# A gated two-mixer block on one core: new places in the queues for modulations, split weights and gate loads, and the long convolution's differences taken from a PSUM copy

## The chip, the cores and the metric

One core of a Trainium2 chip. The metric is the device time of one execution in microseconds; of the kernel before there are three, 1468.36, 1468.63 and 1471.03 us, median 1468.63. The engines are PE (TensorE, matrix products), DVE (VectorE), ACT (ScalarE), POOL (GpSimd) and SP (SyncE, which here only starts DMAs). Each engine takes its instructions in order from its own queue.

## The reference

The block takes x (1024 positions by 1024 channels) and a condition c. Cut to what matters:

```python
mod = silu(c) @ w_ada + b_ada                       # sh1, sc1, g1, sh2, sc2, g2
h = rms_norm(x, norm_mix_g) * (1 + sc1) + sh1
b_s, c_s, v_s, v_c, gl_c, gate_br = split(h @ w_in) # 7 x 1024 columns
y_a = (b_s * causal_dwconv(c_s * v_s, conv_short_w)) @ w_short_out   # 3 taps
u = causal_dwconv(v_c * sigmoid(gl_c), conv_conf_w) + conv_conf_b    # 31 taps
y_b = silu(layer_norm(u, conf_ln_g, conf_ln_b)) @ w_conf_out
g_a, g_b = split(sigmoid(gate_br))
x = x + g1 * ((g_a * y_a + g_b * y_b) @ w_o)
h2 = rms_norm(x, norm_ffn_g) * (1 + sc2) + sh2
a, bgate = split(h2 @ w_ffn_in)
x = x + g2 * ((silu(a) * bgate) @ w_ffn_out)
return rms_norm(x, final_norm_g)
```

## The kernel before

Channels lie on the 128 partitions, positions along the free axis, in halves of 512 columns (`H`). Every matrix product is done in fp32r with a high and a low part of each operand, in three matmuls: high by high, low by high, high by low (L504, L505, L507). A weight is loaded by SP into one of five `raw` buffers (pools `rawp` and `rawbp`), `split_w` casts it to `wh` on ACT (L243) and subtracts to get `wl` on DVE or POOL (L244); there are three buffers of each, so a weight can be split about two products ahead of its use. Loads of raw wait for the split that last used the buffer.

Products come in groups of seven, named "1265734" in that order (a scheme that replaces eight block products by seven, with sums of blocks). Each product is 24 matmuls into two PSUM banks, which ACT and DVE then evacuate ("evac"): ACT copies those of "1", "6" and "5", DVE adds or multiplies those of "2", "7", "3" and "4".

The stages in time:

- The input projection, to about 570 us, in 18 "duals" `d`, each of seven products that yield two streams of 128 channels (`PAIRS`: u, p, q and g streams). Beside it run, on DVE: the long convolution, eight blocks `j` of 45 taps each (`conv`, from dual 1 to dual 12); the short convolution (`short_conv`, L854 on ACT and L857 on DVE), whose steps for the p streams of one dual are issued late, in the next dual, and work in a PSUM bank `x` that is the next dual's `z`, needed first by its product "5"; and modulations (`modulation_of`, L485), each a reduction over a 128x1024 block of w_ada that SP loads, two in each of the duals 3 to 9, at the products named in `MOD_AT`.
- `w_short` products (to about 648 us), then the `w_conf` products, in the order `CONF_ORDER`, which interleaves two groups `d`; their operands `z1` to `z7` are made tile by tile from `cv` by `z_first`, `z_5`, `z_6` and so on: DVE forms `t2z`, ACT casts it to `z6h`, DVE subtracts to `z6l`. The weights of "5", "7" and "3" are sums of two blocks, made by a DMA that accumulates onto `raw` from POOL's queue (`add` in `conf_units`, L397); that of "6" is summed on DVE (L407). On the same POOL queue `gates_b` loads gate tiles `gb` (L1421), and finished tiles go out from it by the accumulating `ma<-gb` (L1394).
- `w_o` and the feed-forward part, which the change does not touch.

The long convolution of block j: `ev` and `od` are the even and odd positions of `u[j]`, `d = ev - od` and `e` the same shifted by one (tile `diff`, one buffer, L1149 and L1150). It gathers odd taps into PSUM accumulators `a0` and `a1` (tiles `c0`, `c1`, two buffers in all), then 15 taps on `e` into c1, and 16 on `d` into c0. Each tap is pinned behind the evac of a product by `read_at(conv_at(...))`. When a block is done, `add_conv` adds it into `tot` on POOL (L1189).

The order on an engine is set by a list scheduler; `tc.issue_after(ins)` pins what is issued within it behind the named instruction in that order.

Of the kernel before, what the change touches and what calls it, by code (L numbers as in the profile page):

```python
# [38 lines left out]
ALU = mybir.AluOpType  # L39
# [4 lines left out]
H = 512  # L44
# [23 lines left out]
BEGUN = 2  # L68
# [33 lines left out]
GATED = 10  # L102


CONV_FROM, CONV_DUALS = 1.0, 11.06

# [8 lines left out]
PRODUCTS = "1265734"  # L117
# [2 lines left out]
CONF_ORDER = [(d, m) for m in "1256" for d in range(2)] + [(0, "3")] + [(d, m) for m in "74" for d in range(2)] + [(1, "3")]  # L120


MOD_FROM, MOD_AT = 16, "53"

# [12 lines left out]
def block_kernel(ctx: ExitStack, tc: tile.TileContext, x0, xT, c, vecs, ada, w_first, w_plain, w_duals,  # L139
                 w_short, w_conf, w_o, w_fi, w_fo0, w_fo1, outT):  # L140
    nc = tc.nc
# [16 lines left out]
    rawp = pool("raw", 3)  # L158
# [8 lines left out]
    rawbp = pool("raw_b", 2, side="right")  # L167
# [4 lines left out]
    def ps2_tile(name):  # L172
        return ps2p.tile([P, H], F32, tag="ps2", name=name)
# [205 lines left out]

        return {m: (lambda m=m: unit(m)) for m in PRODUCTS}  # L380

    conf_homes = [rawp, rawbp, rawp]

    def conf_units(mats, d):


        a = {}
        mat = dict(zip(("11", "12", "21", "22"), mats))

        def get(b, home=None):  # L390
            if home is None:
                conf_homes.append(conf_homes.pop(0))
                home = conf_homes[-1]
            return load(mat[b], home=home)

        def add(raw, b):
            nc.gpsimd.dma_start(raw, mat[b], accum_op=ALU.add)  # L397
            return raw

        def unit(m):  # L400
            if m == "5":
                raw = a["s1"] = add(get("22"), "21")
            elif m == "6":
                lo = split_w.lo
                raw = a["s2"] = get("11", (rawp, rawbp)[d])
                with tc.issue_after(lo):
                    nc.vector.tensor_tensor(raw, raw, a["s1"], ALU.add)  # L407
            elif m == "7":
                raw = add(get("21"), "11")
            elif m == "3":  # L410
                raw = add(a["s2"], "12")
            else:
                raw = get({"1": "11", "2": "12", "4": "22"}[m])
            return split_w(raw, 1024)

        return {m: (lambda m=m: unit(m)) for m in PRODUCTS}

# [432 lines left out]
    def short_conv(j, p, banks):  # L850

        sc[j] = uc_tile(f"sc{j}", T)
        for h, ps in enumerate(banks):
            nc.scalar.activation(ps, p[:, h * H : (h + 1) * H], AF.Copy, scale=col(V_SW, j))  # L854
        for h, ps in enumerate(banks):
            for s in range(1, SK):
                nc.vector.scalar_tensor_tensor(  # L857
                    out=ps if s < SK - 1 else sc[j][:, halves[h]], in0=p[:, h * H + s : (h + 1) * H + s],
                    scalar=col(V_SW + s * KC, j), in1=ps, op0=ALU.mult, op1=ALU.add,
                )  # L860


    reads = []

    def plus(out, ps, b):
        plus.ins = nc.vector.tensor_tensor(out, ps, b, ALU.add).ins
# [16 lines left out]
    def win_evac(d, pairs, banks):  # L883

        st = [{} for _ in pairs]

        def start(e, kind, j):
            if kind == "u":
                u.append(u_tile(j))
                e["b"] = [u[j][:, CK - 1 + h * H : CK - 1 + (h + 1) * H] for h in range(2)]  # L890
            elif kind == "p":
                e["p"] = uc_tile(f"p{j}", T + SK - 1)
                nc.vector.memset(e["p"][:, : SK - 1], 0.0)
                e["b"] = [e["p"][:, SK - 1 + h * H : SK - 1 + (h + 1) * H] for h in range(2)]
            else:
                e["b"] = [None, g_tile("v")]

        def begin():

            rows = uc_tile("sig", T)  # L900
            for i, e in enumerate(st):
                e["t"] = uc_tile("sig", T)
                e["b"], e["c"] = [None, rows[:, halves[i]]], [e["t"][:, s] for s in halves]
                nc.sync.dma_start(e["c"][0], part_dram[d, i])

        def bring(i):
            nc.scalar.copy(banks["x", i], st[i]["c"][0])

        def evac(i, m, ps):
            plus.ins = None  # L910
            read(i, m, ps)
            if plus.ins:
                late_by = 2 * max(0, d - GATED + 1)
                reads.append((d + (2 * (PRODUCTS.index(m) - late_by) + i + 1) / (2 * len(PRODUCTS)), plus.ins))

        def read(i, m, ps):
            kind, j, *rest = pairs[i]
            e = st[i]
            if m in "165":
                if m == "5":  # L920
                    e["z"] = e["c"][1] if kind == "g" else g_tile("z")
                copy = nc.scalar.copy({"1": banks.get(("y", i)), "6": e.get("b", [0, 0])[1], "5": e.get("z")}[m], ps)
                if i:
                    run_late(copy.ins)
            elif m == "2":
                start(e, kind, j)
                if kind == "q":
                    times(sc[j][:, halves[0]], ps, sc[j][:, halves[0]])
                else:
                    nc.scalar.copy(e["b"][0], ps)  # L930
            elif m == "7":
                z = banks["y", i] if kind == "q" else e["z"]
                plus(z, ps, e["z"])
                if kind == "g":
                    late.append(lambda: nc.scalar.activation(z, z, AF.Sigmoid, scale=-1.0))
                elif kind == "q":
                    minus_times(sc[j + 1][:, halves[1]], z, sc[j + 1][:, halves[1]])
            elif m == "3":
                b, z = e["b"][1], e["z"]
                if kind == "u":  # L940
                    nc.scalar.activation(z, z, AF.Sigmoid, scale=-1.0)
                plus(b if kind == "g" else ps, ps, b)
                if kind == "u":
                    times(b, ps, z)
                elif kind == "p":
                    minus_times(b, ps, z)
                elif kind == "q":
                    times(sc[j][:, halves[1]], ps, sc[j][:, halves[1]])
                else:
                    late.append(lambda: nc.scalar.activation(b, b, AF.Sigmoid))  # L950
            elif kind == "u":
                nc.scalar.activation(ps, ps, AF.Sigmoid, scale=-1.0)
                times(e["b"][0], ps, e["b"][0])
            elif kind == "p":
                minus_times(e["b"][0], ps, e["b"][0])
                late.append(lambda: short_conv(j, e["p"], [banks["x", p] for p in range(2)]))
            elif kind == "q":
                minus_times(sc[j + 1][:, halves[0]], ps, sc[j + 1][:, halves[0]])
                for n in range(2):
                    q_store(j + n)  # L960
            else:
                nc.scalar.activation(e["c"][0], ps, AF.Sigmoid, scale=-1.0)
                def store():
                    nc.scalar.dma_start(gate_dram[j][:, halves[1]], e["b"][1])
                    nc.scalar.dma_start(gate_dram[rest[0]], e["t"])
                late.append(store)
        evac.begin, evac.bring = begin, bring
        return evac
# [163 lines left out]
    def conv_at(j):  # L1132
        return CONV_FROM + j * CONV_DUALS / KC
# [5 lines left out]
    def read_at(t):  # L1139

        return max((r for r in reads if r[0] <= t), key=lambda r: r[0])[1]

    def conv(j):
        eo = u[j].rearrange("p (n two) -> p n two", two=2)
        ev, od = eo[:, :, 0], eo[:, :, 1]
        diff = diffp.tile([P, T + CK - 1], F32, tag="diff", name="diff")
        d, e = diff[:, :NE], diff[:, NE : 2 * NE - 1]
        with tc.issue_after(read_at(conv_at(j))):
            nc.vector.tensor_tensor(d, ev, od, ALU.subtract)  # L1149
            nc.vector.tensor_tensor(e, ev[:, 1:], od[:, : NE - 1], ALU.subtract)  # L1150
        a0, a1 = ps2_tile("c0"), ps2_tile("c1")
        n = 0

        def tap(out, src, s, wt, acc):
# [80 lines left out]
    for d, m in win_order:  # L1235
# [8 lines left out]
        if d + 1 < BEGUN and m == PRODUCTS[-1]:  # L1244
            for p in range(2):
                nc.scalar.copy(win_banks[d + 1]["x", p], m1[2 * (d + 1) + p])
        mod_raw = load(ada[MOD_FROM + n_mod], home=dual_units.home) if m in MOD_AT and BEGUN < d < GATED else None
        with tc.issue_after(mm3.ins) if (d, m) == (0, "6") else ExitStack():
            product(win_banks[d], m, th[m], win_evacs[d], onto="2")
        if (d, m) == win_order[0]:  # L1250
# [5 lines left out]
                nc.gpsimd.memset(tot[h], 0.0)  # L1256
        if win_order.index((d, m)) >= len(win_order) - 7:
            q_steps.pop(0)()
        if mod_raw is not None:
            with tc.issue_after(mm3.ins):  # L1260
                modulation_of(MOD_FROM + n_mod, mod_raw)
            n_mod += 1
    while late:
        late.pop(0)()
# [151 lines left out]
    def gates_b(d, m):  # L1416
        row, h = {"2": (0, 0), "7": (1, 1), "3": (0, 1), "4": (1, 0)}.get(m, (0, None))
        for i in range(2 * (h is not None)):
            j = 4 * d + 2 * i + row
            gbs[j, h] = g_tile("gb")  # L1420
            nc.gpsimd.dma_start(gbs[j, h], gate_dram["b", j][:, halves[h]])  # L1421

    yb_banks = [{} for _ in range(2)]
    for p in range(2):
# [571 lines left out]
```

## Time and profile before

| | before |
|---|---|
| runs, us | 1468.36, 1468.63, 1471.03 (median 1468.63) |
| profiled execution, us | 1469.08 |
| its span, first to last instruction, us | 1467.3 |
| mean granted PE clock | 0.992 |
| busy: PE, DVE, ACT, POOL | 98%, 83%, 44%, 36% |
| long-conv taps on DVE (L1158, of diff) | 232 of 746 ns |
| weight splits on POOL (L244) | 78 of 2494 ns |

The profiled execution is one run, 0.45 us above the median; 1.78 us of it lie outside the span. PE is busy nearly always, so what matters is where it is not: a wait's row names the instruction that ended it. A row of the timeline gives the start, the duration, the engine, the line and operation, out<-in, the shape, the count, and in brackets the engine's idle time before it with what ended that. PE rows show overlapping durations (0.39 us, while a matmul starts every 0.223 us).

### The profile page before, as it was taken

What the parts mean: (1) busy time and instruction counts of PE and PEld (TensorE: products, weight loads), DVE (VectorE), ACT (ScalarE), POOL (GpSimd) and SP (SyncE); (2) the same over time, 40 slices, a digit from 0 to 9 for tenths busy, and PEclk for the clock granted to TensorE, in tenths of its full rate; (3) what the DMA queues carried; (4) which work ended last, traced back from release to release, by engine and by line L of the source; (5) the groups of instructions that cost most, each with busy time, mean ns of one, the idle gap of its engine ahead of it and who ended that gap; (6) DMA issues with size and microseconds to landing.
All of it is one profiled execution on the core that took longest, in us unless ns stands there. A gap on an engine that the chain in (4) does not pass through costs nothing.

```text
span 1467.3 us, 17736 instructions
## 1 busy us (share of the span) xinstructions
PE 1436.7 (98%) x6322; PEld 1177.6 (80%) x6322; DVE 1215.4 (83%) x1665; ACT 652.4 (44%) x955; POOL 522.6 (36%) x496
## 2 busy tenths in 40 slices
PE   9999999999989999997999999999999999999997
PEld 4888888777878888886788888888888888888887
DVE  7987999899989999987897799877776666866676
ACT  4873333333333446565535465444444443322235
POOL 0017776776676562012221001110111015663405
PEclk9999999999999999998999999999999999999999
DMA  9743133232335569768694536655554449996903
GB/s 354 274 153 99 59 125 105 101 115 101 125 106 181 165 205 323 218 201 184 165 332 163 172 115 217 218 176 174 173 183 144 150 143 350 390 371 194 356 1 115
DMA packets 95946, 275.04 MB, mean 187 GB/s; under 512 B 10945, under 2 KB 12993, under 8 KB 95858
## 3 DMA queue, kind: packets, MB, share of 16 engines
q1 hardware_dynamic: 46672, 148.92, 30.0%
q0 software_dynamic: 44000, 111.36, 25.1%
q10 hardware_dynamic: 5186, 13.64, 2.4%
q8 instruction: 49, 0.80, 0.2%
q14 instruction: 39, 0.32, 0.1%
HBM read 203.09 MB, written 67.63 MB: 185 GB/s over the span
## 4 chain that ended last, share of the span: by engine, by line
PE 84%; DVE 6%; POOL 4%; issue 2%; DMA 2%; ACT 0%; POOLq 0%; DVEq 0%; ACTq 0%
PE bank L504 10%; PE bank L505 10%; PE bank L507 10%; PE x L507 8%; PE x L505 8%; PE x L504 8%; PE z L507 4%; PE z L505 4%; PE z L504 4%; PE y L505 2%; PE y L504 2%; PE y L507 2%; PE mix L505 2%; PE mix L504 2%; PE mix L507 2%
## 5 line engine op out<-in xcount | busy, mean ns | idle before, releaser
L243 ACT CAST wh<-raw 128x1024 fp32r<-128x1024 f32 (+2 forms) x254 | 262.9, 1037 | 423.9 <-PE bank L505 139.0
L244 DVE TENSOR_TENSOR wl<-raw,wh 128x1024 fp32r<-128x1024 f32 (+2 forms) x176 | 212.4, 1208 | 52.9 <-ACT wh L243 51.1
L244 POOL TENSOR_TENSOR wl<-raw,wh 128x1024 fp32r<-128x1024 f32 x78 | 194.2, 2494 | 112.4 <-ACT wh L243 112.4
L1158 DVE SCALAR_TENSOR_TENSOR c<-diff,vec,c 128x512 f32<-128x512 f32 x232 | 164.3, 746 | 1.0
L1634 POOL DMA_DIRECT2D hid<-stage x70 | 37.4, 535 | 342.6 <-DVE stage L553 322.5
L504 PE MATMUL bank<-th,wh 128*128 128x512 f32 x336 | 132.5, 394 | 10.1 <-DVE sc L857 10.1
L507 PE MATMUL bank<-th,wl 128*128 128x512 f32 x336 | 132.0, 393 | 0.0
L505 PE MATMUL bank<-tl,wh 128*128 128x512 f32 x336 | 131.7, 392 | 0.0
L504 PEld LDWEIGHTS bank<-th,wh 128*128 128x128 f32 x336 | 63.9, 190 | 25.0 <-DVE sc L857 11.7
L505 PEld LDWEIGHTS bank<-tl,wh 128*128 128x128 f32 x336 | 63.9, 190 | 13.3
L507 PEld LDWEIGHTS bank<-th,wl 128*128 128x128 f32 x336 | 63.6, 189 | 13.4
L1158 DVE SCALAR_TENSOR_TENSOR c<-u,wsum,c 128x512 f32<-128x512 f32 x96 | 69.7, 746 | 0.6
L504 PE MATMUL x<-th,wh 128*128 128x512 f32 x176 | 68.5, 389 | 0.0
L505 PE MATMUL x<-tl,wh 128*128 128x512 f32 x176 | 68.5, 389 | 0.0
L507 PE MATMUL x<-th,wl 128*128 128x512 f32 x176 | 68.4, 390 | 0.0
L552 ACT CAST stage<-g 128x512 fp32r<-128x512 f32 x60 | 37.3, 621 | 58.9 <-DMA hid<-stage 37.7
L553 DVE TENSOR_TENSOR stage<-g,stage 128x512 fp32r<-128x512 f32 x60 | 41.2, 688 | 24.8 <-ACT stage L552 24.6
L1658 POOL DMA_DIRECT2D th<-hid x77 | 41.1, 534 | 51.8 <-PE x L507 28.0
L485 DVE CUSTOM_DVE_ANT_0 raw<-raw,cs,vec 128x1024 f32<-128x1024 f32 x24 | 42.7, 1783 | 11.8 <-DMA raw<-in_ada 11.0
L1658 POOL DMA_DIRECT2D tl<-hid x77 | 41.2, 535 | 19.0 <-DMA tl<-hid 3.2
L264 DVE TENSOR_TENSOR raw<-raw 128x1024 f32<-128x1024 f32 (+1 forms) x15 | 17.8, 1187 | 31.4 <-DMA raw<-in_w_fi 19.0
L504 PE MATMUL bank<-t2h,wh 128*128 128x512 f32 x112 | 43.6, 389 | 0.0
(830 smaller groups left out, 4156.6 us busy)
## 6 DMA issues: line engine op xcount, KB each, us to landing
hid<-stage POOLq DMA_DIRECT2D x70, 512.0 KB, 4.5
raw<-in_w_duals SPq DMA_DIRECT2D x65, 512.0 KB, 3.7
raw<-in_w_fi SPq DMA_DIRECT2D x54, 512.0 KB, 4.5
th<-hid POOLq DMA_DIRECT2D x77, 256.0 KB, 5.9
tl<-hid POOLq DMA_DIRECT2D x77, 256.0 KB, 5.9
ada<-in_ada SPq DMA_DIRECT2D x24, 512.0 KB, 5.5
raw<-in_ada SPq DMA_DIRECT2D x24, 512.0 KB, 4.3
raw<-in_w_fo SPq DMA_DIRECT2D x16, 512.0 KB, 6.1
```

The source lines that it names most:

```text
L243: hi = nc.scalar.copy(wh, raw)
L244: lo = lo_engine.tensor_tensor(wl, raw, f32(wh), ALU.subtract)
L264: eng.tensor_tensor(a["s1"], a["21"], a["22"], ALU.add)
L485: nc.vector.tensor_tensor_reduce(out=raw, in0=raw, in1=cs, scale=1.0, scalar=col(V_ADA, b), op0=ALU.mult, op1=ALU.add, accum_out=modc(b),)
L504: nc.tensor.matmul(ps, wh, xh, start=first, stop=False, skip_group_check=again)
L505: nc.tensor.matmul(ps, wh, xl, start=False, stop=False, skip_group_check=again)
L507: mm3.ins = nc.tensor.matmul(ps, wl, xh, start=False, stop=last, skip_group_check=again).ins
L552: t_split.act = nc.scalar.copy(hi, src).ins
L553: t_split.ins = nc.vector.tensor_tensor(lo, src, f32(hi), ALU.subtract).ins
L1158: tap.ins = nc.vector.scalar_tensor_tensor(out=out, in0=src[:, s : s + H], scalar=wt, in1=acc, op0=ALU.mult, op1=ALU.add).ins
L1634: nc.gpsimd.dma_start(hid_dram[key], s)
L1658: nc.gpsimd.dma_start(t, hid_dram[key][:, s])
```

## The change

Four edits. The long convolution's odd positions are first copied by ACT into c1 in PSUM (512 columns), pinned behind an evac copy 0.2 of a convolution before its start; DVE makes the first 512 columns of both differences from that copy, POOL the remaining 15 and 14 columns from SBUF. The two modulations of a dual are both issued at product "5" and pinned behind the last short-conv tap. A `w_conf` weight, except those of "1" and "2", is split behind the last operand split issued (`split`). The gate loads `gb` are pinned behind the last accumulating weight load issued.

```diff
+OD_EARLY = 0.2
-MOD_FROM, MOD_AT = 16, "53"
+MOD_FROM = 16
...
     def conf_units(mats, d):
         def add(raw, b):
-            nc.gpsimd.dma_start(raw, mat[b], accum_op=ALU.add)
+            conf_adds.append(nc.gpsimd.dma_start(raw, mat[b], accum_op=ALU.add).ins)
             return raw
...
-            return split_w(raw, 1024)
+            return split_w(raw, 1024, () if m in "12" else (split.act, split.ins))
...
     def short_conv(j, p, banks):
...
-                nc.vector.scalar_tensor_tensor(
+                short_conv.ins = nc.vector.scalar_tensor_tensor(
...
-                )
+                ).ins
...
+    def copy_at(t):
+        return max((r for r in copies if r[0] <= max(t, copies[0][0])), key=lambda r: r[0])[1]
+
     def conv(j):
...
+        a0, a1 = ps2_tile("c0"), ps2_tile("c1")
+        with tc.issue_after(copy_at(conv_at(j - OD_EARLY))):
+            nc.scalar.copy(a1, od[:, :H])
+        nc.gpsimd.tensor_tensor(d[:, H:], ev[:, H:], od[:, H:], ALU.subtract)
+        nc.gpsimd.tensor_tensor(e[:, H:], ev[:, 1 + H :], od[:, H : NE - 1], ALU.subtract)
         with tc.issue_after(read_at(conv_at(j))):
-            nc.vector.tensor_tensor(d, ev, od, ALU.subtract)
-            nc.vector.tensor_tensor(e, ev[:, 1:], od[:, : NE - 1], ALU.subtract)
-        a0, a1 = ps2_tile("c0"), ps2_tile("c1")
+            nc.vector.tensor_tensor(d[:, :H], ev[:, :H], a1, ALU.subtract)
+            nc.vector.tensor_tensor(e[:, :H], ev[:, 1 : 1 + H], a1, ALU.subtract)
...
     for d, m in win_order:
-        mod_raw = load(ada[MOD_FROM + n_mod], home=dual_units.home) if m in MOD_AT and BEGUN < d < GATED else None
...
-        if mod_raw is not None:
-            with tc.issue_after(mm3.ins):
-                modulation_of(MOD_FROM + n_mod, mod_raw)
+        for n in range('55'.count(m) * (BEGUN < d < GATED)):
+            with tc.issue_after(short_conv.ins):
+                modulation_of(MOD_FROM + n_mod, load(ada[MOD_FROM + n_mod], home=(dual_units.home,dual_units.home)[n_mod % 2]))
             n_mod += 1
...
     def gates_b(d, m):
...
-            nc.gpsimd.dma_start(gbs[j, h], gate_dram["b", j][:, halves[h]])
+            with tc.issue_after(conf_adds[-1]) if conf_adds else ExitStack():
+                nc.gpsimd.dma_start(gbs[j, h], gate_dram["b", j][:, halves[h]])
```

How the instructions stand, at the three places where the rows differ most. First DVE in dual 3, where the second long convolution (u_592) begins and the short convolution's taps (L857) follow. `ISA raw,mod` is a modulation. Before:

```order
L1158 SCALAR_TENSOR_TENSOR u_589<-diff,vec,c_4088 128x512
L1158 SCALAR_TENSOR_TENSOR c_4144<-u_592,wsum,c_4144 128x512
L1149 TENSOR_TENSOR diff<-u_592 128x527
L1150 TENSOR_TENSOR diff<-u_592 128x526
L1158 SCALAR_TENSOR_TENSOR c_4144<-u_592,wsum,c_4144 128x512
L485 ISA raw,mod<-raw,cs,vec 128x1024
L485 ISA mod 128x1
L1158 SCALAR_TENSOR_TENSOR c_4145<-u_592,wsum,c_4145 128x512
L1158 SCALAR_TENSOR_TENSOR c_4144<-u_592,wsum,c_4144 128x512
L857 SCALAR_TENSOR_TENSOR bank<-p_1001,vec,bank 128x512 x2
L857 SCALAR_TENSOR_TENSOR sc_1568<-p_1001,vec,bank 128x512 x2
L869 TENSOR_TENSOR sc_1381<-bank,sc_1381 128x512
```

And now, the same taps and what follows them:

```order
L1168 SCALAR_TENSOR_TENSOR c_4145<-u_592,wsum,c_4145 128x512
L858 SCALAR_TENSOR_TENSOR bank<-p_1001,vec,bank 128x512 x2
L858 SCALAR_TENSOR_TENSOR sc_1568<-p_1001,vec,bank 128x512 x2
L870 TENSOR_TENSOR sc_1381<-bank,sc_1381 128x512
L707 MEMSET u_1605 128x30
L486 ISA raw,mod<-raw,cs,vec 128x1024
L486 ISA mod 128x1
L486 ISA raw,mod<-raw,cs,vec 128x1024
L486 ISA mod 128x1
L894 MEMSET p_1834 128x2
```

The modulation that stood ahead of the short-conv taps now stands behind them, with the dual's second one right after it.

Next ACT among the `w_conf` products "5" and "6", where operands and weights are cast. `wh` is a weight's high part, `z5h`, `z6h`, `z3h` are operand tiles, `vz` evacuations, `cv` the swish. Before:

```order
L243 CAST wh<-raw 128x1024
L1275 ACTIVATE cv_4941<-cv_4941,vec 128x512
L1401 COPY vz<-bank 128x512 x2
L243 CAST wh<-raw 128x1024
L544 CAST z6h<-t2z 128x512
L1275 ACTIVATE cv_4987<-cv_4987,vec 128x512
L243 CAST wh<-raw 128x1024
L544 CAST z6h<-t2z 128x512
L1401 COPY vz<-y 128x512 x2
L544 CAST z6h<-t2z 128x512 x2
```

And now:

```order
L244 CAST wh<-raw 128x1024
L1284 ACTIVATE cv_4965<-cv_4965,vec 128x512
L1410 COPY vz<-bank 128x512 x2
L545 CAST z6h<-t2z 128x512
L1284 ACTIVATE cv_5011<-cv_5011,vec 128x512
L545 CAST z6h<-t2z 128x512
L244 CAST wh<-raw 128x1024
L1410 COPY vz<-y 128x512 x2
L545 CAST z6h<-t2z 128x512 x2
L244 CAST wh<-raw 128x1024
```

Each of the two later weights is cast one or two operand casts further back.

Last POOL's queue at the same place: gate loads (`gb`), accumulating weight loads (`raw<-in_w_conf`) and the tiles that go out (`ma<-gb`). Before:

```order
L397 DMA raw<-in_w_conf 128x1024
L1394 DMA ma_4669<-gb 128x512
L1394 DMA ma_4683<-gb 128x512
L1421 DMA gb<-gate_b_120 128x512
L1421 DMA gb<-gate_b_119 128x512
L1394 DMA ma_4731<-gb 128x512
L1394 DMA ma_4745<-gb 128x512
L1421 DMA gb<-gate_b_121 128x512
L1421 DMA gb<-gate_b_123 128x512
L397 DMA raw<-in_w_conf 128x1024 x2
L1421 DMA gb<-gate_b_125 128x512
L397 DMA raw<-in_w_conf 128x1024
```

And now:

```order
L1431 DMA gb<-gate_b_118 128x512
L1403 DMA ma_4693<-gb 128x512
L1403 DMA ma_4707<-gb 128x512
L1431 DMA gb<-gate_b_120 128x512
L1403 DMA ma_4755<-gb 128x512
L1403 DMA ma_4769<-gb 128x512
L398 DMA raw<-in_w_conf 128x1024 x2
L1431 DMA gb<-gate_b_119 128x512
L1431 DMA gb<-gate_b_121 128x512
L1431 DMA gb<-gate_b_123 128x512
L1431 DMA gb<-gate_b_125 128x512
L398 DMA raw<-in_w_conf 128x1024
```

The two weight loads now go ahead of the gate loads that wait for the tiles going out.

More of the change, by code (lines that the diff above doesn't have):

```diff
@@ L380, in added_units @@
         return {m: (lambda m=m: unit(m)) for m in PRODUCTS}
-    conf_homes = [rawp, rawbp, rawp]
+    conf_homes, conf_adds = [rawp, rawbp, rawp], []
     def conf_units(mats, d):
@@ L856, in short_conv @@
             for s in range(1, SK):
-                nc.vector.scalar_tensor_tensor(
+                short_conv.ins = nc.vector.scalar_tensor_tensor(
                     out=ps if s < SK - 1 else sc[j][:, halves[h]], in0=p[:, h * H + s : (h + 1) * H + s],
                     scalar=col(V_SW + s * KC, j), in1=ps, op0=ALU.mult, op1=ALU.add,
-                )
-    reads = []
+                ).ins
+    reads, copies = [], []
     def plus(out, ps, b):
@@ L922, in read @@
                 copy = nc.scalar.copy({"1": banks.get(("y", i)), "6": e.get("b", [0, 0])[1], "5": e.get("z")}[m], ps)
+                copies.append((d + (2 * PRODUCTS.index(m) + i + 1) / (2 * len(PRODUCTS)), copy.ins))
                 if i:
```

## The prediction

> **What bounds the kernel now.** I read the page first, then PE's waits, then PE in stretches of 25 us, and only then the engines around each stall. On the page: the engines' busy shares, and who owns the chain that ended last.
>
> ```profile
> PE 1436.7 (98%) x6322; PEld 1177.6 (80%) x6322; DVE 1215.4 (83%) x1665; ACT 652.4 (44%) x955; POOL 522.6 (36%) x496
> PE 84%; DVE 6%; POOL 4%; issue 2%; DMA 2%; ACT 0%; POOLq 0%; DVEq 0%; ACTq 0%
> ```
>
> PE is the bound. The change leaves PE's instructions as they are, so it can only win what PE loses by standing still or by a lowered clock, and can only lose by new stalls. PE's waits name the two largest groups (total us, times, longest):
>
> ```profile
> PE bank L504 <- DVE sc L857: 10.1, 4, 4.8
> PE bank L504 <- ACT z6h L544: 8.4, 1, 8.4
> ```
>
> Each stretch of 25 us gives PE's busy time, its matmuls and the granted clock. An undisturbed one holds 112 matmuls, so one costs 25/112 = 0.223 us and a product of 24 takes 5.36 us.
>
> ```profile
> 250.00:275.00 25.00, 23.26 (x103) 1.00 0.16 52
> 300.00:325.00 25.00, 23.26 (x103) 1.00 0.42 148
> 325.00:350.00 25.00, 25.00 (x112) 1.00 0.12 43
> 350.00:375.00 25.00, 23.22 (x95) 0.93 0.29 106
> 425.00:450.00 25.00, 20.21 (x83) 0.93 0.55 191
> 675.00:700.00 25.00, 16.63 (x64) 0.80 0.83 190
> 700.00:725.00 25.00, 24.76 (x107) 1.00 0.59 157
> ```
>
> The four stretches with short-conv stalls lack 9 + 9 + 17 + 29 = 64 matmuls, 14.3 us, more than the 10.1 us of waiting because the clock also drops. Around 691 us 48 + 5 are missing, 10.7 and 1.1 us. Together 117 matmuls, 26.1 us: the most that this change can win.
>
> **Modulations: what they hold up.** DVE and PE rows at the short-conv stalls (start, duration, instruction, idle time before it and its cause):
>
> ```profile
> 268.92 2.60 DVE L485 CUSTOM_DVE_ANT_0 raw<-raw,cs,vec 128x1024 f32<-128x1024 f32 x1 [3.77 <-DMA raw<-in_ada]
> 308.39 3.23 DVE L485 CUSTOM_DVE_ANT_0 raw<-raw,cs,vec 128x1024 f32<-128x1024 f32 x1
> 349.08 2.71 DVE L485 CUSTOM_DVE_ANT_0 raw<-raw,cs,vec 128x1024 f32<-128x1024 f32 x1
> 273.42 1.40 DVE L857 SCALAR_TENSOR_TENSOR sc<-p,vec,bank 128x512 f32<-128x512 f32 x2
> 274.21 0.50 PE L504 MATMUL bank<-th,wh 128*128 128x512 f32 x1 [1.74 <-DVE sc L857]
> 426.71 1.29 DVE L485 CUSTOM_DVE_ANT_0 raw<-raw,cs,vec 128x1024 f32<-128x1024 f32 x1 [3.76 <-DMA raw<-in_ada]
> 433.26 3.37 DVE L485 CUSTOM_DVE_ANT_0 raw<-raw,cs,vec 128x1024 f32<-128x1024 f32 x1
> 436.56 0.73 DVE L857 SCALAR_TENSOR_TENSOR sc<-p,vec,bank 128x512 f32<-128x512 f32 x1
> ```
>
> PE waits for the bank that the last short-conv tap reads. A modulation stands ahead of those taps in DVE's queue, and twice DVE also waits for its DMA. The change keeps all 14 modulations and puts both of a dual behind the short conv's last tap. At 274.21 that takes 3.77 + 2.60 = 6.4 us from ahead of a stall of 1.74; at 437 it takes 3.76 + 1.29 + 3.37 = 8.4 from ahead of 4.8. The other two stalls share the remaining 10.1 − 4.8 − 1.74 = 3.6 us, 1.8 each, and lose 3.23 and 2.71 ahead of them. So each stall is covered, two by a microsecond or so. Nothing else moves ahead of the taps except conv taps, which the third part makes cheaper. I take the whole 14.3 and give back 0.5 (none to 4 us, if the two narrow ones stay). What goes behind: two modulations in a row, 2.6 to 6.6 us by these rows, now delay the evacuation adds of product "7", and the loads that wait for their buffers on SP. Their cover is the rest of that product, 5.36 us, and the next bank; weight loads stood behind a modulation before as well, and at 437 the modulations now end earlier, not later. The wait for the DMA shrinks too, since the load is issued before the taps and consumed after them. Price zero; uncovered it is rival three.
>
> The trace has its own price of a lowered clock, a stretch behind the 1.78 us stall near 354 (us, busy, matmuls, clock):
>
> ```profile
> 355.00:357.50 2.50, 2.50 (x7) 0.51 0.39 159
> ```
>
> Half the rate for about 2.5 us. [...]
>
> **Edges of the summed weights and the gates' loads: the stall at 691.** Rows of POOL, DVE, ACT and PE there:
>
> ```profile
> 681.27 0.57 POOL L1421 DMA_DIRECT2D gb<-gate_b  x1 [5.17 <-DMA ma<-gb]
> 682.83 1.84 POOL L397 DMA_DIRECT2D raw<-in_w_conf  x2
> 675.98 1.22 DVE L244 TENSOR_TENSOR wl<-raw,wh 128x1024 fp32r<-128x1024 f32 x1
> 681.25 0.68 DVE L557 SCALAR_TENSOR_TENSOR t2z<-cv,cv 128x512 f32<-128x512 f32 x1
> 689.97 1.04 ACT L243 CAST wh<-raw 128x1024 fp32r<-128x1024 f32 x1 [9.26 <-DMA raw<-in_w_conf]
> 690.92 0.61 ACT L544 CAST z6h<-t2z 128x512 fp32r<-128x512 f32 x1
> 693.51 0.62 ACT L544 CAST z6h<-t2z 128x512 fp32r<-128x512 f32 x1 [1.00 <-DVE t2z L557]
> 695.92 0.62 ACT L544 CAST z6h<-t2z 128x512 fp32r<-128x512 f32 x1 [1.79 <-DVE t2z L557]
> 691.59 1.22 PE L504 MATMUL bank<-z6h,wh 128*128 128x512 f32 x2 [8.37 <-ACT z6h L544]
> ```
>
> A chain of queues: POOL waits 5.17 us to load a gate into a buffer still being written out; the accumulating weight load behind it goes out at 682.83; its sum reaches ACT at 689.97; the second z6h cast stands behind that weight's cast; PE waits 8.37 us. The change cuts it twice. The casts wh of "6" go behind z6h, so the second z6h starts when its t2z ends, 681.25 + 0.68 = 681.93, and ends at 682.55, before PE needs it (691.59 − 8.37 = 683.22). And the gate load goes behind the weight loads, which then wait for the split that frees their buffer (675.98 + 1.22 = 677.2), go out 5.6 us earlier and land by the same delay (689.97 − 682.83 = 7.1) near 684.3.
>
> What is late next: z6h three and four. They followed the second by 2.6 and 5.0 us (693.51 − 690.92, 695.92 − 690.92), paced by DVE's t2z chain, so they would end near 685.1 and 687.5. PE uses a tile in 6 matmuls, 1.34 us, and would want them at 684.6 and 685.9 (or 1.34 after the third). That leaves about 0.5 + 1.1 = 1.6 us, or 2.8 with z6l behind z6h. I take 2.0, bounds 0 and 5 (a half-rate stretch on top). The deferred wh cast comes about 689 and its wl 1.2 us later, with its product two products after 681: 681.2 + 10.7 = 691.9. The gates' loads, now later, are read some products on; cover enough by these starts, but the thinnest of this part.
>
> **Long conv: what is cheaper on DVE.** Groups and rows: the two differences, the nearest subtract-sized operation with a PSUM operand, ACT's copy, a difference beside POOL, the taps, the running sum on POOL and POOL's weight split.
>
> ```profile
> L1149 DVE TENSOR_TENSOR diff<-u 128x527 f32<-128x527 f32 x8 | 11.8, 1476 | 0.0
> L1150 DVE TENSOR_TENSOR diff<-u 128x526 f32<-128x526 f32 x8 | 11.6, 1447 | 0.0
> L866 DVE TENSOR_TENSOR z<-bank,z 128x512 f32<-128x512 f32 x16 | 10.9, 683 | 2.4 <-PE bank L507 2.2
> L922 ACT COPY z<-bank 128x512 f32<-128x512 f32 x20 | 11.7, 583 | 18.0 <-PE bank L507 15.4 <-DVE u L1158 2.7
> 239.91 1.80 DVE L1150 TENSOR_TENSOR diff<-u 128x526 f32<-128x526 f32 x1
> 241.11 5.23 POOL L244 TENSOR_TENSOR wl<-raw,wh 128x1024 fp32r<-128x1024 f32 x2
> L1158 DVE SCALAR_TENSOR_TENSOR c<-diff,vec,c x232: 719/745/757, 142.1 to 547.6; 128x512 f32<-128x512 f32 x116
> 360.97 7.34 DVE L1158 SCALAR_TENSOR_TENSOR c<-diff,vec,c 128x512 f32<-128x512 f32 x11
> 238.12 3.02 POOL L1189 TENSOR_TENSOR tot<-tot,u 128x512 f32<-128x512 f32 x2 [5.78 <-DVE u L1158]
> L244 POOL TENSOR_TENSOR wl<-raw,wh 128x1024 fp32r<-128x1024 f32 x78 | 194.2, 2494 | 112.4 <-ACT wh L243 112.4
> 300.00:550.00 250.00, 241.69 (x1051) 198.85 (x1050) 241.08 (x334) 93.77 (x133) 165.10 (x74) 0.99 0.45 144
> ```
>
> Differences now cost DVE 8 × (1476 + 1447) ns = 23.4 us; 16 at 683 ns would be 10.9. Saving 12.4 us, bounds 0 (if the new form is stretched as the old) and 12.4; I take 12.4, because the taps, which also read one operand in PSUM, hold 719 to 757 ns over 232 while POOL runs. [...]
>
> Against it: c1 is taken from the start, so a conv no longer interleaves with the tail of the one before, and about 16 more neighbouring taps depend on each other. A tap alone takes 0.745 us, a run of 11 only 0.667 each (7.34/11): 16 × 0.08 = 1.3 us more, 2 if such pairs are slower than one tap. DVE was busy 241.1 of 250 us, so it has been near its limit, and gets about 10 us of room. PE never waited for the long conv itself, so I count nothing for this part; its effect is that DVE reaches the short conv no later although PE runs 14 us faster.
>
> ACT gets 8 copies of 0.58 us, 4.7 us, hidden by its 44% load. Each waits for the conv before to release c1: its last e tap lies 16 d taps before that conv's end, 10.7 us, and the copy is asked for 9 taps before the next start, so DVE may run 4.7 us late before ACT waits, and the weights cast behind it are two products ahead. POOL gets 16 small subtractions. Bounds 0.05 us each (15/512 of a tot add) and 1.5 (a whole one); I take 0.5, a microsecond per conv, hidden by the 112.4 us in which POOL waits for casts. Their own wait is a rival. I put 0.5 us for all of it.
>
> **The sum.** −14.3 − 10.7 − 1.1 + 0.5 + 2.0 + 0.5 = −23.1 us. The profiled execution took 1469.08 (span 1467.3 and 1.78 around it), so 1446.0; the median of the runs is 0.45 below that execution, so about 1445.5. I say 1446.
>
> **Rivals.** No change means within 0.2%, 2.9 us; less can't be told here.
>
> One: only one group of stalls goes. If z6's pace, the deferred cast or the later gate loads hold PE as long as before, the short conv's part remains: 1468.6 − 14.3 + 0.5 = 1455. If DVE is late for the short conv anyway, the other: 1468.6 − 11.8 + 2 = 1459. For it: two stalls were covered by about a microsecond, and the z6 path keeps a thin cover. Against it: the named waits stand wholly in what is moved. 17%.
>
> Two, slower: POOL. Its subtractions read what the previous conv's last tap leaves, and at some starts stand one weight split ahead of the tot adds, behind which POOL already waited 5.78 us. One product earlier the wait is W = 5.8 + 5.4 = 11.1 us at worst, and the splits behind it are late. Their cover is two products less a split, 10.7 − 2.5 = 8.2 us. Each microsecond beyond costs PE one per conv: 1446 + 8 × (W − 8.2). At W = 11.1 this gives 1469; it decides from 11.5 (over 1472); at 13 it is 1484. Against it: POOL's wait of 5.78 cost PE nothing, and its splits wait for casts anyway. 9%.
>
> Three, nothing: the stalls only move, evacuation "7" waiting behind two modulations in seven duals for 2 to 3 us each, and z6 as forecast gone but paid back so: 1468.6 − 23 + 7 × 3 = 1467. 5%.
>
> Mine: 66%. Better than 1443: 3%, since 26.1 is all there is. From 1443 to 1459 lie my case (alone 1443 to 1451) and most of rival one: 8 in 10. Faster 0.86, same 0.05, slower 0.09.
>
> **What would show it.** PE's waits no longer name sc of the short conv, and z6h by less than 3 us; the stretches above hold about 110 matmuls; the new differences take about 0.69 us; POOL's added waits stay under 8 us. I am wrong if PE's list names wl or wh, an evacuated bank at "7", or z6 tiles for over 5 us, or if the clock drops in a new stretch.

## The result, and the profile after

The changed kernel takes 1443.59 us (median of four runs, 1442.39 to 1444.08), the kernel before beside it 1468.49: ratio 0.9827, 95% interval 0.981 to 0.9844, 25 us less. The profiled execution took 1443.7 (span 1441.9). The page's busy shares and the owners of its last chain now read:

```profile
PE 1428.6 (99%) x6322; PEld 1173.5 (81%) x6322; DVE 1198.8 (83%) x1665; ACT 655.2 (45%) x963; POOL 522.0 (36%) x512
PE 97%; POOL 1%; DVE 0%; issue 0%; POOLq 0%
```

PE's waits, and the stretches of 25 us that were short before:

```profile
PE clock L721 <- ACT sq L668: 1.9, 1, 1.9
PE clock L721 <- DVE ones_r L739: 1.6, 1, 1.6
PE clock L721 <- DVE newton L780: 0.7, 1, 0.7
...
250.00:275.00 25.00, 25.00 (x112) 1.00 0.29 93
300.00:325.00 25.00, 25.00 (x112) 1.00 0.40 126
350.00:375.00 25.00, 25.00 (x112) 1.00 0.22 82
425.00:450.00 25.00, 25.00 (x112) 1.00 0.70 221
675.00:700.00 25.00, 25.00 (x111) 1.00 0.83 225
700.00:725.00 25.00, 25.00 (x112) 1.00 0.90 246
```

Both large waits are gone; what is left are three short ones in the first 17 us. Of the 117 missing matmuls all but one are back, at the full granted clock. DVE at the first of the old stalls, and the new differences:

```profile
264.44 1.41 DVE L858 SCALAR_TENSOR_TENSOR bank<-p,vec,bank 128x512 f32<-128x512 f32 x2
265.75 1.40 DVE L858 SCALAR_TENSOR_TENSOR sc<-p,vec,bank 128x512 f32<-128x512 f32 x2
267.68 1.28 DVE L486 CUSTOM_DVE_ANT_0 raw<-raw,cs,vec 128x1024 f32<-128x1024 f32 x1
269.44 2.86 DVE L486 CUSTOM_DVE_ANT_0 raw<-raw,cs,vec 128x1024 f32<-128x1024 f32 x1 [0.48 <-issue]
...
L1160 DVE TENSOR_TENSOR diff<-u,c x8: 677/683/687, 127.9 to 494.6; 128x512 f32<-128x512 f32 x8
```

The short conv's taps end at 267.2, before PE wants their bank, and the two modulations follow them.

### The profile page after: what moved, and what is told of

The parts are those of the page before. It is cut to its first block, busy times and chain, and to the rows that moved or that the text cites. A ratio compares the mean times of both kernels' runs of the same rounds, so it can differ in the third digit from the quotient of the medians.

```text
span 1441.9 us, 17770 instructions
## 1 busy us (share of the span) xinstructions
PE 1428.6 (99%) x6322; PEld 1173.5 (81%) x6322; DVE 1198.8 (83%) x1665; ACT 655.2 (45%) x963; POOL 522.0 (36%) x512
## 4 chain that ended last, share of the span: by engine, by line
PE 97%; POOL 1%; DVE 0%; issue 0%; POOLq 0%
PE bank L506 14%; PE bank L505 14%; PE bank L508 14%; PE x L508 8%; PE x L506 8%; PE x L505 8%; PE z L506 4%; PE z L508 4%; PE z L505 4%; PE y L508 3%; PE y L506 3%; PE y L505 3%; PE mix L506 2%; PE mix L508 2%; PE mix L505 2%; PE lead L501 1%
## 5 line engine op out<-in xcount | busy, mean ns | idle before, releaser
L1168 DVE SCALAR_TENSOR_TENSOR c<-u,wsum,c 128x512 f32<-128x512 f32 x96 | 66.8, 750 | 0.8
L265 DVE TENSOR_TENSOR raw<-raw 128x1024 f32<-128x1024 f32 (+1 forms) x15 | 17.8, 1188 | 36.4 <-DMA raw<-in_w_fi 24.1
L486 DVE CUSTOM_DVE_ANT_0 raw<-raw,cs,vec 128x1024 f32<-128x1024 f32 x24 | 39.1, 1639 | 9.5 <-DMA raw<-in_ada 5.4
```

Of the source, the lines that this page charges most:

```text
L265: eng.tensor_tensor(a["s1"], a["21"], a["22"], ALU.add)
L486: nc.vector.tensor_tensor_reduce(out=raw, in0=raw, in1=cs, scale=1.0, scalar=col(V_ADA, b), op0=ALU.mult, op1=ALU.add, accum_out=modc(b),)
L1168: tap.ins = nc.vector.scalar_tensor_tensor(out=out, in0=src[:, s : s + H], scalar=wt, in1=acc, op0=ALU.mult, op1=ALU.add).ins
```

## The experiments

Each was timed beside the kernel before, whose medians were 1467.19, 1468.09 and 1467.47 us in the three groups of four. Each kernel has four runs, the gate loads alone ten. "Less" is the ratio's distance from 1 times that median.

| kernel | us, median (range) | ratio (95%) | less, us |
|---|---|---|---|
| modulations alone | 1461.37 (1458.96 to 1462.34) | 0.9956 (0.9941 to 0.997) | 6.5 |
| long conv alone | 1458.59 (1457.77 to 1459.98) | 0.994 (0.9925 to 0.9955) | 8.8 |
| weights' split alone | 1456.71 (1455.3 to 1457.9) | 0.9925 (0.9908 to 0.9941) | 11.0 |
| gate loads alone | 1465.05 (1462.95 to 1466.66) | 0.9981 (0.9972 to 0.999) | 2.8 |
| split and gate loads | 1457.64 (1456.73 to 1458.11) | 0.9929 (0.9913 to 0.9946) | 10.4 |
| all but modulations | 1448.13 (1447.29 to 1449.13) | 0.9867 (0.9852 to 0.9882) | 19.5 |
| all but long conv | 1448.77 (1448.14 to 1449.59) | 0.9871 (0.9856 to 0.9886) | 18.9 |
| all, differences from SBUF | 1446.91 (1444.24 to 1448.9) | 0.9857 (0.9842 to 0.9872) | 21.0 |
| all, long conv in one block only | 1442.32 (1442.13 to 1442.83) | 0.9829 (0.9815 to 0.9844) | 25.1 |
| all, one difference from SBUF | 1442.4 (1442.27 to 1443.11) | 0.983 (0.9816 to 0.9845) | 24.9 |
| all, differences made twice | 1454.66 (1453.5 to 1455.87) | 0.9915 (0.9899 to 0.9932) | 12.5 |
| all but gate loads | 1443.59 (1442.71 to 1443.88) | 0.9836 (0.9822 to 0.9851) | 24.1 |
| the change | 1443.59 (1442.39 to 1444.08) | 0.9827 (0.981 to 0.9844) | 25.4 |

**Modulations alone.** Into the kernel before went only this part:

```diff
-            with tc.issue_after(mm3.ins):
-                modulation_of(MOD_FROM + n_mod, mod_raw)
+            with tc.issue_after(short_conv.ins):    # both of a dual, at product "5"
+                modulation_of(...)
```

> The kernel before with the modulations' new place alone. Theory A (each part lifts its own stall): the four waits of PE for the short conv's sc go, worth 64 matmuls; 1468.5 - 14.3 + 0.5 = 1454.7 us, the wait of 8.4 us for z6h stays. Theory B (the short-conv stalls are DVE's load, of which the modulations are only a part): the two narrow stalls near 312 and 354 stay, 9 + 17 matmuls = 5.8 us, so about 1460 us.

PE's waits, the stretch that is now short, and a DVE row ahead of it:

```profile
PE bank L504 <- ACT z6h L544: 7.0, 1, 7.0
PE bank L504 <- DVE sig L866: 3.8, 1, 3.8
...
425.00:450.00 25.00, 25.00 (x112) 1.00 0.68 206
450.00:475.00 25.00, 21.23 (x85) 0.91 0.55 165
475.00:500.00 25.00, 25.00 (x107) 0.96 0.51 184
...
441.95 7.98 DVE L1150 TENSOR_TENSOR diff<-u 128x526 f32<-128x526 f32 x1
```

All four waits for sc are gone, as theory A had it, but the time is nearer to B's. A new wait of 3.8 us for an evacuation (`sig`) appears at 471, and with the lowered clock takes back 27 + 5 matmuls, 7.1 of the 14.3 us. Ahead of it one difference of the long conv lasts 7.98 us.

**Long conv alone.**

```diff
+            nc.scalar.copy(a1, od[:, :H])
+        nc.gpsimd.tensor_tensor(d[:, H:], ...)   # 15 columns, and e: 14
-            nc.vector.tensor_tensor(d, ev, od, ALU.subtract)
+            nc.vector.tensor_tensor(d[:, :H], ev[:, :H], a1, ALU.subtract)   # and e
```

> The kernel before with the long convolution's differences through PSUM alone. Theory A: the modulations still stand ahead of the short conv's taps and two of them still wait for their DMA, so PE's waits for sc stay within 1 us of 10.1 in total; 1467 to 1469 us. Theory B: DVE gets 12 us of room, comes earlier to the modulations, and the two narrow stalls go: 1468.5 - 5.8 = about 1462.7 us. In both, a difference takes about 0.68 us.

PE's waits, then the modulation at the first old stall and the one at the last (DVE), and POOL's running sum ahead of the first; below them the first one's load, on SP, before and in this kernel:

```profile
PE bank L505 <- ACT z6h L545: 8.7, 1, 8.7
PE bank L505 <- DVE sc L858: 3.6, 1, 3.6
...
263.88 1.28 DVE L486 CUSTOM_DVE_ANT_0 raw<-raw,cs,vec 128x1024 f32<-128x1024 f32 x1 [2.55 <-POOL wl L245]
423.15 3.38 DVE L486 CUSTOM_DVE_ANT_0 raw<-raw,cs,vec 128x1024 f32<-128x1024 f32 x1
...
234.03 2.55 POOL L1199 TENSOR_TENSOR tot<-tot,u 128x512 f32<-128x512 f32 x2 [2.81 <-DVE u L1168]
```

```profile
264.50 7.38 SPq L227 DMA_DIRECT2D raw<-in_ada  x2
```

```profile
260.26 5.27 SPq L228 DMA_DIRECT2D raw<-in_ada  x2
```

More than theory B: three of the four stalls go with the modulations still ahead of the taps. The first modulation starts at 263.9 instead of 268.9. Its load went out 4.2 us earlier, since SP holds that load until POOL's split frees the buffer (here the split ends at 260.23), and POOL was ahead by about as much: the running sum, which waits for DVE's last tap, starts at 234.03 instead of 238.12, after four differences that took DVE 2.7 us instead of 6.5. The row puts the last of the modulation's own wait to another of POOL's splits and not to the load; which of the two it was isn't settled. Only the stall at 427 is left, where a modulation stands between two of the taps.

**Weights' split alone.**

```diff
-            return split_w(raw, 1024)
+            return split_w(raw, 1024, () if m in "12" else (split.act, split.ins))
```

> The kernel before with the later split of the w_conf weights alone. Theory A: the second z6h no longer stands behind the weight whose sum lands near 690, and PE takes up its product at once; that weight is cast near 690 and split by 692, just when it is needed (691.9), so 1468.5 - 11.8 + 2.5 = about 1459 us. Rival C: the late sum is the cause whichever cast stands ahead, PE stops one product on for wl or wh, by 3 us or more: 1462 to 1468 us.

ACT's second z6h and the cast of the late sum, and POOL's accumulating loads, still in their old place:

```profile
681.13 0.62 ACT L544 CAST z6h<-t2z 128x512 fp32r<-128x512 f32 x1 [0.99 <-DVE t2z L557]
687.90 1.05 ACT L243 CAST wh<-raw 128x1024 fp32r<-128x1024 f32 x1 [0.19 <-DMA raw<-in_w_conf]
...
681.92 1.84 POOL L397 DMA_DIRECT2D raw<-in_w_conf  x2
```

Theory A, and 2 us better: the sum reaches ACT at 687.9, 2 us earlier than before but still 6 us after the second z6h, and nothing urgent stands behind it. PE has no wait here (110 matmuls from 675 to 700).

**Gate loads alone.**

```diff
+            with tc.issue_after(conf_adds[-1]) if conf_adds else ExitStack():
                 nc.gpsimd.dma_start(gbs[j, h], ...)
```

> The kernel before with the gate loads' new place in POOL's queue alone. Theory A: the accumulating load goes out near 677 instead of 682.8 and lands near 684.3, ACT casts that weight, then z6h ends near 686, so PE waits 2.8 us instead of 8.4 and pays less for its clock: 1468.5 - 7 = about 1461.5 us. Rival D: the sum lands no earlier, because the load waits for something else than the gate load ahead of it (its buffer, or the DMA engines): 1468 us.

POOL's accumulating loads, the weight's cast on ACT, and PE's wait:

```profile
676.37 0.87 POOL L397 DMA_DIRECT2D raw<-in_w_conf  x1 [2.07 <-DVE wl L244]
679.81 0.87 POOL L397 DMA_DIRECT2D raw<-in_w_conf  x1 [2.57 <-DMA raw<-in_w_conf]
685.76 1.04 ACT L243 CAST wh<-raw 128x1024 fp32r<-128x1024 f32 x1 [6.17 <-DMA raw<-in_w_conf]
...
PE bank L504 <- ACT z6h L544: 5.3, 1, 5.3
```

Between A and D. The load near 676 that I meant is the other of the pair; the one that ACT waits for has its own first half to wait for, and goes out at 679.8. The z6 wait falls from 8.4 to 5.3 us.

**Both edges without the rest**, and **all but the gate loads**:

> The kernel before with the weights' later split and the gate loads' new place together, without the other two parts. Theory A: the stall at z6 goes whole, 53 matmuls = 11.8 us, less up to 2 us of z6's own pace: 1457 to 1459 us; PE's waits for sc of the short conv stay at about 10 us. If the stall is one chain that either edge cuts, this equals the better of the two alone.

> The changed kernel with the gate loads back at their old place in POOL's queue. Since the split's new place alone won the whole of the z6 stall and both edges together no more: 1443.6 us within 1.5, and no wait for z6h, wh or wl. If the gate loads matter once PE arrives 14 us earlier at this stage, PE waits again there: 1446 us or more.

The two together give 10.4 us, the split alone 11.0; without the gate loads the whole change takes the same 1443.59 us, with two waits of PE, of 0.5 and 0.4 us, at the next operand (z3). So the gate loads' new place is worth nothing that can be measured once the split has moved. It is one chain, and either cut helps, the split's cut wholly.

**All but modulations**:

> The changed kernel with the modulations back where they stood before. Theory A: the short-conv stalls are back, 14.3 us: 1443.6 + 14.3 = about 1458 us. Theory B: with the cheaper differences two of the four stalls are gone, so only 1443.6 + 8.5 = about 1452 us.

```profile
PE bank L505 <- DVE sc L858: 3.7, 1, 3.7
```

Theory B's side, and beyond it: one stall returns, the one at 427, and the modulations' place is worth 5.9 us (25.4 less 19.5), not 14.3.

**All but long conv**:

> The changed kernel with the long convolution's differences back on DVE from SBUF. Theory A: PE never waited for the long conv; 1443.6 to 1445 us. Theory B: DVE is 12 us more loaded while PE runs 14 us faster, comes late to the short conv or to an evacuation, and PE waits again: 1448 to 1456 us.

The new wait of PE, the difference on DVE, and POOL's rows beside it:

```profile
471.94 0.80 PE L504 MATMUL bank<-th,wh 128*128 128x512 f32 x1 [3.74 <-DVE sig L866]
...
442.87 7.97 DVE L1150 TENSOR_TENSOR diff<-u 128x526 f32<-128x526 f32 x1
...
442.71 2.74 POOL L244 TENSOR_TENSOR wl<-raw,wh 128x1024 fp32r<-128x1024 f32 x1
445.07 2.86 POOL L1189 TENSOR_TENSOR tot<-tot,u 128x512 f32<-128x512 f32 x2
447.57 2.70 POOL L244 TENSOR_TENSOR wl<-raw,wh 128x1024 fp32r<-128x1024 f32 x1
```

Theory B by the time, but not by its reason alone. One difference, 0.69 us when undisturbed, starts 0.2 us after POOL begins four instructions without a gap, and ends at 450.84, half a microsecond after they do (447.57 + 2.70 = 450.27). DVE comes out 7 us late and has no idle time from there to 471, where PE waits for its `sig`. In the kernel before, the same difference missed POOL's run:

```profile
454.96 0.69 DVE L1150 TENSOR_TENSOR diff<-u 128x526 f32<-128x526 f32 x1
```

**All, differences from SBUF.** Everything of the change stays, but for the operand:

```diff
-            nc.vector.tensor_tensor(e[:, :H], ev[:, 1 : 1 + H], a1, ALU.subtract)
+            nc.vector.tensor_tensor(e[:, :H], ev[:, 1 : 1 + H], od[:, :H], ALU.subtract)   # and d
```

> The changed kernel, but DVE's two differences read the odd positions from SBUF instead of the copy in PSUM; the copy is still made, and read by nothing before it is overwritten. Lock theory: with two SBUF operands beside POOL's work a difference again takes over 1.2 us in the mean, up to some 2.9; with one operand in PSUM it is 0.68. Length theory (the earlier form was slow because of its 527 columns or its strides): 0.68 to 0.72 us. The time, by theory A, 1443.6 to 1445 us; by theory B, up to 10 us more.

```profile
L1160 DVE TENSOR_TENSOR diff<-u x8: 677/852/2585, 126.7 to 489.8; 128x512 f32<-128x512 f32 x8
L1161 DVE TENSOR_TENSOR diff<-u x8: 678/700/7640, 128.5 to 490.4; 128x512 f32<-128x512 f32 x8
...
PE bank L505 <- DVE sig L867: 2.1, 1, 2.1
```

The durations are the lock theory's, over 1.2 us in the mean, and the longest is beyond it: same length, same place, and 677 to 7640 ns (means 1.32 and 1.83, sums 10.6 and 14.7 us) instead of 677 to 687. That it is POOL's work that holds a difference is read from the times of the rows; no run takes that work away. It isn't that the changed kernel's differences miss POOL: beside 15 of its 16, POOL has an instruction under way, not counting DMA issues. The 7.64 us falls at 443, and PE waits near 470 again, 2.1 us.

**One block in the new form; one difference in the old.**

```diff
+        if j == 6:      # the new form; all other blocks as before
```
```diff
+            nc.vector.tensor_tensor(e[:, :H], ev[:, 1 : 1 + H], od[:, :H] if j == 6 else a1, ALU.subtract)
```

> The changed kernel with the differences back on DVE from SBUF as before in seven of the eight blocks; only the seventh block (whose second difference took 7.97 us in the kernel without this part) keeps the new form. Lock theory (one difference held for 8 us behind POOL's unbroken run is what PE feels 20 us later): PE's wait of 3.7 us for sig near 470 is gone, 1443.6 to 1445.5 us. Load theory (the sum of DVE's time counts): an eighth of the part's worth, so about 1448 us.

> The changed kernel with one of its 16 differences reading its odd positions from SBUF: the second of the seventh block. Lock theory: if POOL's run falls on it, that one takes 5 to 8 us, and PE waits 2 to 4 us for sig near 470; 1446 to 1449 us. Load theory: one difference more or less in the old form changes nothing, 1443.6 us.

The first answers: with the other seven blocks' 14 differences in the old form, 11.6 + 10.3 = 21.9 us of DVE time, the whole gain is there, and PE has no wait but the three at the start. Its old differences, in the order of the two lines:

```profile
L1165 DVE TENSOR_TENSOR diff<-u 128x527 f32<-128x527 f32 x7 | 11.6, 1654 | 0.0
L1166 DVE TENSOR_TENSOR diff<-u 128x526 f32<-128x526 f32 x7 | 10.3, 1473 | 0.0
```

With the two new ones that is 23.2 us, about as much as in the kernel before (23.4), so DVE's time in sum isn't what makes PE wait near 470. The seventh block's two differences also start earlier here, at 436.6 and 437.8, where the held ones of the two kernels above started at 442.87 and 443.18; so this kernel shows that PE's wait goes when the hold goes; that with the operand in PSUM there is no hold is shown by the kernel above, beside the change: 7.64 us there, 0.68 in the change.

The second does not answer. Its one old difference, and POOL at that moment:

```profile
441.44 0.68 DVE L1161 TENSOR_TENSOR diff<-u 128x512 f32<-128x512 f32 x1
...
441.01 0.92 POOL L435 DMA_DIRECT2D raw<-in_w_duals  x1 [0.31 <-POOL wl L245]
441.64 0.55 POOL L1157 TENSOR_TENSOR diff<-u 128x15 f32<-128x15 f32 x1
...
442.74 2.41 POOL L245 TENSOR_TENSOR wl<-raw,wh 128x1024 fp32r<-128x1024 f32 x1 [0.38 <-ACT wh L244]
```

POOL was issuing a DMA and then made its 15 columns, and the difference took 0.68 us. The condition in its expectation was not met, and the time is the change's own. It ended at 442.12, 0.6 us ahead of POOL's next weight split; the held ones started 0.2 and 0.3 us after such a split (442.87 after 442.71, 443.18 after 442.87). Less than a microsecond lies between the two.

**Differences made twice**:

```diff
+            for _ in range(2):
                 nc.vector.tensor_tensor(d[:, :H], ev[:, :H], a1, ALU.subtract)   # and e
```

> The changed kernel with each of the 16 differences issued twice (the second overwrites the first with the same numbers). That gives DVE back 16 x 0.68 = 10.9 us of the 12.4 it was spared, evenly, and without two SBUF operands. Load theory: the stall near 470 returns, about 1447 to 1449 us. Lock theory: no long hold, 1.4 us a block, 1443.6 to 1445 us.

Neither theory. No hold (no difference over 0.69 us) and no wait near 470, but 11 us slower than the change. PE waits for another `sig`, at 523, and then for POOL's sum; the wait for `sig`, DVE's last tap, the sum, and PE's wait for it:

```profile
PE bank L505 <- DVE sig L867: 1.8, 1, 1.8
...
567.16 0.75 DVE L1169 SCALAR_TENSOR_TENSOR u<-diff,vec,c 128x512 f32<-128x512 f32 x1
...
568.34 2.79 POOL L1200 TENSOR_TENSOR tot<-tot,u 128x512 f32<-128x512 f32 x2
...
569.96 3.78 PE L1209 MATMUL mu<-tot,ones 128*128 128x512 f32 x4 [4.61 <-POOL tot L1200]
...
550.00:575.00 25.00, 20.39 (x76) 0.87 0.90 265
```

The last tap, at 543.55 in the changed kernel, comes at 567.16, and the layer norm's mean, which PE takes from tot, stops PE. The delay is 23.6 us for 10.9 us of added work: near the end some taps now also stand behind the next stage's operand splits in DVE's queue. The two waits cost 16 matmuls from 500 to 550 and 36 from 550 to 575, 11.6 us. So with enough added to DVE, evenly and without a hold, a `sig` comes late too: this kernel doesn't refute the load theory, it shows other deadlines of it. That the kernel with one block in the new form has 23.2 us of differences, against 21.8 here, and its last tap at 532.8 speaks for the order as the larger cause, but no run separates the two.

## Why the prediction was right, and where not

- **The total.** Forecast −23.1, measured −25 us; 1446 against 1443.6. The count of missing matmuls, 117 or 26.1 us, was the right bound, and nearly all of it came.
- **z6: right in mechanism, residual over-sized.** I gave back 2.0 us for z6h three and four; measured none. I took 6 matmuls a tile, as one product uses. The trace has 16 high-by-high matmuls for four tiles, so 48 in three kinds, 12 a tile: PE interleaves the two "6" products, and the third tile is wanted later.

```profile
L505 PE MATMUL bank<-z6h,wh x16: 389/389/498, 667.3 to 677.7; 128*128 128x512 f32 x16
```

- **The gate loads.** I had the chain cut twice; the second cut is worth 2.8 us alone and nothing beside the first, and I dated its load 3 us too early (677.2; it went at 679.8) by taking the wrong one of two.
- **The short conv's 14.3 us: right in sum, wrong in whose it is.** The step that failed is "I count nothing for this part" on the long conv, and with it the 14.3 for the modulations. Alone the modulations' place gives 6.5 and the long conv 8.8 us; taken out of the whole they cost 5.9 and 6.5 (4.5 and 5.2 by the medians alone; each of these figures is known to some 2 us). That the total came out is in part luck: the change happened to hold the part that I had put at nothing. The modulations do lift all four waits, but then the differences fall at other times, one takes 7.98 us, and 7.1 us are lost again at an evacuation. My rival three had that shape, a stall that moves, but blamed two modulations in a row, which no run shows.
- **DVE's price of a difference** was right, 0.683 us in the median, and with it the choice of the whole 12.4 us: with both operands in SBUF, all else as in the change, the 16 took up to 7.64 us, with one in PSUM 0.687 at most. What I drew from it was wrong: that 12.4 us less on DVE move nothing on PE. Alone, DVE's earlier taps bring POOL's sum and with it the modulation's load forward by 4 us. With the modulations moved, what counts is the longest difference, 8 us, which the kernel before does not have (2.9 us).
- **The slower rival, POOL,** did not come. Its small subtractions waited 7.6 us in all, ACT's copies of 0.626 us 7.0, and PE waited for neither; a subtraction took about 0.215 us in the median against my 0.5.

## What to carry to other kernels

Count what the bound engine lacks in each stretch, in its own instructions: that gave the total here to 2 us, clock included. But to say which edit wins it, ask of each edit alone what the next-late thing is; two causes ahead of the same wait share its price. And value a contended operation by its longest hold at the worst place, not only by its mean: the longest may not be in the trace that you have.

## What the runs showed of the hardware

A DVE subtraction with two SBUF operands took 7.97 us in one kernel (all but long conv) and 7.64 in another (all, differences from SBUF), in each beside four POOL instructions that followed each other without a gap (442.71 to 450.27, and 442.87 to 450.26), and ended 0.6 us after the last of them. With the kernel of the 7.64 otherwise the same, an operand in PSUM made it 0.68, at 444.64, beside the start of POOL's same run.

In the kernel before, pauses of PE of 1.74 us ended at 274.21 and 314.32, and the 2.5 us from 274.5 and from 314.5 had a granted clock of 1.00 and 12 matmuls each; pauses of 1.78, 4.79 and 8.37 us ended at 354.48, 437.36 and 691.59, and the 2.5 us from 355, 437.5 and 691.5 had 0.51, 0.50 and 0.50, with 7, 6 and 6 matmuls. Whether the length of the pause decides is not shown.
